# The second half's attention of a two-layer decoder: a stream of two-key-block tiles in a fixed TensorE order

## The chip, the cores and the metric

The kernel runs on one core of a Trainium2 chip. Its engines are TensorE (PE in the profile; PEld is its weight loading), VectorE (DVE), ScalarE (ACT), GpSimd (POOL) and SyncE (SP), whose queue issues nearly all DMAs of this kernel. The metric is the device time of one execution in microseconds (us), the median of several runs.

## What is computed

A decoder trunk of two layers for 1024 tokens of width 1024, all in float32: an mLSTM layer with its MLP, then a multi-head latent attention (8 heads) with its MLP. The attention shares its keys and values, and each head has a part without rotation (128) and a rotary part (64) that all heads' keys share:

```python
def block(args):
    qn_b, qr_b, start = args
    s = (jnp.einsum('bqhd,bkhd->bhqk', qn_b, k_nope)
         + jnp.einsum('bqhd,bkd->bhqk', qr_b, k_rope)).astype(jnp.float32) * scale
    qpos = start + jnp.arange(B_QBLOCK, dtype=jnp.int32)
    s = jnp.where(kpos[None, :] <= qpos[:, None], s, -jnp.inf)
    p = jax.nn.softmax(s, axis=-1)
    return jnp.einsum('bhqk,bkhd->bqhd', p.astype(v.dtype), v)
...
def sqrelu_mlp(h, w1, w2):
    return jnp.square(jax.nn.relu(h @ w1)) @ w2
```

## The kernel before

Matrix products are made of three matmuls on parts: each float32 operand is split into a rounded high part (ACT's cast) and a low part (DVE's subtraction), and `mm3` (L279 to L282) multiplies high by high, high by low and low by high. `wsplit` (L235) does this for weights that arrive by DMA in a `raw` tile, `split_mod` (L498) for results in PSUM.

The tokens are worked in two halves of 512. While one half goes through the latent attention, the MLP of the other half runs beside it. `two_streams` (L2779) weaves the two generators: it takes a step of the attention side, which says by the number it yields how many MLP steps are due, and then takes that many from the MLP side. 0 means none, 0.5 half a step. `go` (L2762) runs each step under `issue_after` the last TensorE instruction before it, so that TensorE's instructions of one step come after those of the steps before. Within a step the planner of the framework chooses the order on each engine, by priority and by its own estimate of times; `prompt` (L244) raises the priority.

An MLP step of layer 1's first half (`mlp`, L1297) is 24 matmuls of 512 columns: a hidden block of 128 (`hidden`, into a `ps` tile of PSUM) or a share of the output (`up_rows`, into `pm` tiles). Each step can stop in its middle, at `yield "within"`, and each has one 512 KB weight transfer, asked for two steps ahead (`AHEAD`).

The change is in the attention of the second half, whose queries see up to 1024 keys. Its unit is a pair of query tiles of one head (`j` = 2 or 3): the query tiles 2j and 2j+1 of 128 queries each, with `nk` = 6 or 8 key blocks of 128. For each head `loaded_head` (L1877) fetches keys, query, rotary query and values from DRAM into `k4` tiles (512 KB each). `attend_beside` (L1981) then does, in turn:

- `scores` (L1803) for both query tiles of a pair, each into a `pm` tile (two PSUM banks; there are two such tiles): `score_mm` makes five matmuls for each 512 keys and adds the causal mask; `softmax` takes the row maximum on DVE, the exponential with its row sum on ACT, the reciprocal and the scaling on DVE. Probabilities go to `raw` tiles, of which there are four, shared with the weights of the MLP.
- `turned` (L1984): TensorE transposes the probabilities of four key blocks into two `pc` tiles of PSUM, and `split_mod` splits them into two `hd` tiles (there are eight).
- `products` (L2000): these tiles times the values, summed over the key blocks in a `ps` tile, one round behind `turned`.

A pair has two rounds of up to four key blocks. In each round, products of the round before, transposes, and in the last round also the scores of the next pair form one step. The MLP steps due after the rounds are 1, 0.5 and 0.5 in rotation (L2171).

The rotary keys are the tiles `hf.kk`: high and low part, two `hd` tiles of 1024 columns for the second half, whose first halves are fetched from DRAM (L1650 to L1653) and whose second halves `latent` computes (L1688, L1689). Once the last pair's scores are done, `load_o` (L2188) fetches the outputs of heads 0 to 5 for the output projection; from head 6 on they stay in SBUF (`last_o`, L2182).

Of the kernel before, what the change touches and what calls it, by code (L numbers as in the profile page):

```python
# [9 lines left out]
F32 = mybir.dt.float32  # L10
F32R = mybir.dt.float32r
# [71 lines left out]
def kernel(  # L83
# [1528 lines left out]
    def latent(hf, behind):  # L1612
# [35 lines left out]
        for i in range(2):  # L1648
            nc.sync.dma_start(hf.cs[:, i], rope_d[i][:, ts(hf.i, H)])
        if hf.i:  # L1650
            hf.kk = [hd(F32R), hd(F32R)]
            for i in range(2):
                nc.sync.dma_start(hf.kk[i][:, 0:H].bitcast(F32), kkd[i])  # L1653
        else:
            t = hdv(F32R)
            hf.kk = [t[:, 0], t[:, 1]]
# [29 lines left out]
        kr = last_of(rp)  # L1686
        rstd_k = last_of(rs)
        nc.scalar.copy(hf.kk[0][:, s], kr)  # L1688
        nc.vector.tensor_sub(hf.kk[1][:, s], kr, hf.kk[0][:, s].bitcast(F32))  # L1689
        if not hf.i:  # L1690
            for i in range(2):
                nc.sync.dma_start(kkd[i], hf.kk[i].bitcast(F32))
# [84 lines left out]
    def score_mm(o2, kk, q, kn, i):  # L1777
# [5 lines left out]
        for g in range((n + 511) // 512):  # L1783
            w = min(512, n - g * 512)
            o = o2(g)
            ks = slice(g * 512, g * 512 + w)
            kh, kl = kn[0][:, ks], kn[1][:, ks]
            nc.tensor.matmul(o[:, :w], ql, kh, start=True, stop=False)  # L1788
            nc.tensor.matmul(o[:, :w], qh, kl, start=False, stop=False)
            nc.tensor.matmul(o[:, :w], qT, kk[1][:, ks], start=False, stop=False)  # L1790
            nc.tensor.matmul(o[:, :w], qT, kk[0][:, ks], start=False, stop=False)
            if g == i // 4:
                nc.tensor.matmul(o[:, ts(i % 4, P)], identb, maskA, start=False, stop=False)
            nc.tensor.matmul(o[:, :w], qh, kh, start=False, stop=True)  # L1794

    def softmax(f, pr, n):
        m, l = small(1), small(1)
# [180 lines left out]
                finish()  # L1978
        late()

    def attend_beside(hf, groups, dense, behind=lambda: None):  # L1981


        def turned(work):  # L1984
            PTh, PTl = hdv(F32R, 256), hdv(F32R, 256)
            n = 0
            for u, b0, nb in work:
                for b in range(b0, b0 + nb, 2):
                    pt = pc()
                    turns = [(0, b), (1, b), (0, b + 1), (1, b + 1)]  # L1990
                    if b + 2 == u.nk:
                        turns.pop(2)
                    for m, (i, kb) in enumerate(turns):
                        nc.tensor.transpose(pt[:, ts(m, P)], u.prs[i][:, ts(kb, P)], ident)  # L1994
                    s = slice(n * 256, n * 256 + len(turns) * P)
                    split_mod(flat_of(PTh)[:, s], flat_of(PTl)[:, s], pt[:, : len(turns) * P], None)
                    n += 2
            return PTh, PTl

        def products(work, PT):  # L2000
            n = 0
            for u, b0, nb in work:
                if b0 == 0:
                    u.po = ps()[:, :256]
                for kb in range(b0, b0 + nb):
                    o, at = u.po, slice(0, 256)
                    if kb == u.nk - 1:
                        o, at = u.po[:, P:], slice(0, P)
                    mm3(o, *u.v[kb], PT[0][:, n, at], PT[1][:, n, at], kb == 0, kb == u.nk - 1)
                    n += 1  # L2010
                if b0 + nb == u.nk:
                    s = ts(u.j % 2, 256)
                    if u.hh < 6:
                        o = tmp()[:, :256]
                        nc.scalar.copy(o, u.po)
                        nc.sync.dma_start(oT[ts(u.hh, P), ts(u.j, 256)], o)
                    else:
                        split_mod(hf.o.hi[u.hh][:, s], hf.o.lo[u.hh][:, s], u.po, None)

        def begin():  # L2020
            us = []
            for head, j in next(groups, []):
                u = Half()
                (u.hh, _, _, u.v), u.j, u.nk = head, j, 2 * j + 2
                u.prs = scores(hf.kk, (head, j))
                us.append(u)
            return us

        late = None
        yield "align"  # L2030
        us = begin()
        yield 1
        while us:
            if sum(u.nk for u in us) <= 4:
                rounds = [[(u, 0, u.nk) for u in us]]
            else:
                rounds = [[(u, b, min(4, u.nk - b))] for u in us for b in range(0, u.nk, 4)]
            for n, work in enumerate(rounds):
                if late:
                    late()  # L2040
                PT = turned(work)
                late = lambda a=(work, PT): products(*a)
                if len(rounds) == 1:
                    yield 1
                if n == len(rounds) - 1:
                    us = begin()
                    if not us:
                        behind()
                yield next(dense)
        late()  # L2050

    def attention_first(hf):

# [96 lines left out]
    def attention_second(hf):  # L2150
# [12 lines left out]
        def units():  # L2163
            for hh in range(NH):
# [1 line left out]
                if hh == 6:  # L2166
                    last_o(hf)
                for j in range(2, 4):
                    yield [(h_, j)]

        yield from attend_beside(hf, units(), cycle((1, 0.5, 0.5)), lambda: load_o(hf))  # L2171

    def primed(g, then):

# [771 lines left out]
```

## Time and profile before

| | |
|---|---|
| Median of 3 runs | 2295.67 us |
| Lowest, highest | 2294.85, 2296.79 us |
| Span of the profiled execution | 2291.6 us |
| VectorE busy over the span | 1691.5 us (74%) |
| ScalarE busy over the span | 1126.3 us (49%) |
| HBM read, written | 343.65 MB, 98.57 MB |

The span runs from the first to the last instruction of one profiled execution. A row of the timeline has start, duration, engine, line, operation, output tile and inputs, and, in brackets, how long the engine had been idle before it and what released it. TensorE's matmuls overlap, and the ends shown are modelled, so the distance from one start to the next is read, not the duration. In a group of the rows by form, the numbers behind the bar are busy time and the mean of one instruction in ns, then the idle time ahead of the group and its releaser.

### The profile page before, as it was taken

Reading aid. Unit: us, or ns where it says so; the run is one execution under the profiler, and the core shown is the slowest. Engines: PE = TensorE matmul, PEld = TensorE weight load, DVE = VectorE, ACT = ScalarE, POOL = GpSimd, SP = SyncE. Lnnn points to the kernel's source line nnn. Section 1 sums busy time; section 2 is a strip of 40 time slices with the busy share of each in tenths; the row PEclk is TensorE's granted clock in tenths of the full one; section 3 lists DMA queues with packets and bytes.
Section 4 is the critical chain, followed back from the end, with each engine's and each line's share of the span. In section 5 each row is a group of like instructions: output and inputs, shape, how many; then the busy total and the mean of one; then the engine's idle time right before and its main releaser. Section 6 shows DMA issues by size and latency. Waiting matters only on the chain.

```text
span 2291.6 us, 32039 instructions
## 1 busy us (share of the span) xinstructions
PE 2265.0 (99%) x11818; PEld 1904.4 (83%) x11818; DVE 1691.5 (74%) x2715; ACT 1126.3 (49%) x1915; POOL 84.3 (4%) x164
## 2 busy tenths in 40 slices
PE   8999999999999999999999999999999999999998
PEld 6888888888888878878888888888888888989997
DVE  6677767889887877687765777656666398698776
ACT  4355425865334445545444654444444354655453
POOL 1000000001122210000000000000000000000000
PEclk9999999999999999999999999999999999999999
DMA  9544454668999887666776755764434352546332
GB/s 318 184 128 131 149 166 146 204 218 267 327 280 308 280 297 267 194 221 198 246 235 202 248 189 160 245 233 149 143 102 148 106 157 83 161 142 183 117 111 111
DMA packets 399597, 444.33 MB, mean 194 GB/s; under 512 B 27123, under 2 KB 285232, under 8 KB 399440
## 3 DMA queue, kind: packets, MB, share of 16 engines
q1 hardware_dynamic: 386496, 397.09, 54.7%
q0 software_dynamic: 12944, 45.20, 5.3%
q8 instruction: 93, 1.52, 0.3%
q14 instruction: 64, 0.52, 0.1%
HBM read 343.65 MB, written 98.57 MB: 193 GB/s over the span
## 4 chain that ended last, share of the span: by engine, by line
PE 85%; DVE 5%; DMA 5%; issue 3%; ACT 2%; POOL 0%; SPq 0%; DVEq 0%; ACTq 0%; POOLq 0%
PE ps L280 14%; PE ps L281 13%; PE ps L282 13%; PE pm L281 10%; PE pm L280 10%; PE pm L282 9%; DMA raw<-in_mlp_w_dram 3%; PE pc L281 2%; PE pc L280 2%; PE pc L282 2%; PE pc L1994 1%; DVE k L247 1%; PE pm L1794 1%; DVE wl L239 1%; PE pm L1788 1%
## 5 line engine op out<-in xcount | busy, mean ns | idle before, releaser
L238 ACT CAST wh<-raw 128x1024 fp32r<-128x1024 f32 (+2 forms) x317 | 321.4, 1016 | 417.0 <-PE ps L281 187.5
L239 DVE TENSOR_TENSOR wl<-raw,wh 128x1024 fp32r<-128x1024 f32 (+2 forms) x317 | 375.3, 1186 | 196.2 <-ACT wh L238 175.8
L280 PE MATMUL ps<-k,wh 128*128 128x512 f32 (+1 forms) x1237 | 468.3, 379 | 0.3 <-ACT tmp L533 0.2
L282 PE MATMUL ps<-k,wl 128*128 128x512 f32 (+1 forms) x1237 | 462.1, 374 | 0.0
L281 PE MATMUL ps<-k,wh 128*128 128x512 f32 (+1 forms) x1237 | 461.7, 373 | 0.0
L280 PEld LDWEIGHTS ps<-k,wh 128*128 128x128 f32 x1237 | 233.1, 188 | 44.3 <-issue 3.0
L282 PEld LDWEIGHTS ps<-k,wl 128*128 128x128 f32 x1237 | 233.0, 188 | 41.5
L281 PEld LDWEIGHTS ps<-k,wh 128*128 128x128 f32 x1237 | 233.2, 188 | 40.6 <-issue 1.2
L247 DVE TENSOR_TENSOR k<-k,pm 128x512 f32<-128x512 f32 (+1 forms) x250 | 192.2, 800 | 60.2 <-PE pm L282 59.5
L280 PE MATMUL pm<-wh,hd 128*128 128x512 f32 x488 | 193.0, 395 | 1.7 <-ACT raw L1799 1.5
L282 PE MATMUL pm<-wh,hd 128*128 128x512 f32 x488 | 190.4, 390 | 0.0
L281 PE MATMUL pm<-wl,hd 128*128 128x512 f32 x488 | 190.4, 390 | 0.0
L280 PEld LDWEIGHTS pm<-wh,hd 128*128 128x128 f32 x488 | 91.7, 188 | 22.0 <-ACT raw L1799 2.5
L282 PEld LDWEIGHTS pm<-wh,hd 128*128 128x128 f32 x488 | 91.6, 188 | 19.8 <-DVE hd L502 0.5
L281 PEld LDWEIGHTS pm<-wl,hd 128*128 128x128 f32 x488 | 91.8, 188 | 18.4 <-issue 0.5
L280 PE MATMUL pm<-hd,wk 128*128 128x512 f32 x256 | 101.3, 396 | 1.4 <-ACT hd L501 1.4
L281 PE MATMUL pm<-hd,wk 128*128 128x512 f32 x256 | 100.0, 391 | 0.4 <-DVE hd L502 0.4
L280 PE MATMUL pm<-hd,wh 128*128 128x512 f32 x256 | 99.2, 389 | 0.6 <-ACT hd L501 0.6
L281 PE MATMUL pm<-hd,wh 128*128 128x512 f32 x256 | 99.6, 390 | 0.2 <-DVE hd L502 0.2
L282 PE MATMUL pc<-k,wl 128*128 128x256 f32 (+1 forms) x307 | 99.3, 323 | 0.5 <-DVE wl L239 0.5
L282 PE MATMUL pm<-hd,wk 128*128 128x512 f32 x256 | 99.7, 390 | 0.0
L282 PE MATMUL pm<-hd,wl 128*128 128x512 f32 x256 | 99.7, 390 | 0.0
(502 smaller groups left out, 4701.8 us busy)
## 6 DMA issues: line engine op xcount, KB each, us to landing
raw<-in_mlp_w_dram SPq DMA_DIRECT2D x176, 512.0 KB, 4.7
raw<-in_mlp_w_dram SPq DMA_DIRECT2D x128, 256.0 KB, 4.8
raw<-in_ada_w_dram SPq DMA_DIRECT2D x54, 512.0 KB, 4.7
raw<-in_a_w_in_dram SPq DMA_DIRECT2D x44, 512.0 KB, 4.0
lo<-wl POOLq DMA_DIRECT2D x32, 512.0 KB, 6.2
wk<-lo SPq DMA_DIRECT2D x64, 256.0 KB, 4.2
xs<-k SPq DMA_DIRECT2D x40, 256.0 KB, 4.0
hd<-in_ada_w_dram SPq DMA_DIRECT2D x18, 512.0 KB, 7.9
```

The source lines that it names most:

```text
L238: nc.scalar.copy(hi[:, :n], r[:, :n])
L239: i = nc.vector.tensor_sub(lo[:, :n], r[:, :n], hi[:, :n].bitcast(F32))
L247: return f(*a, **k)
L280: nc.tensor.matmul(o, lh, rh, start=start, stop=False)
L281: nc.tensor.matmul(o, lh, rl, start=False, stop=False)
L282: pe_last[0] = nc.tensor.matmul(o, ll, rh, start=False, stop=stop)
L1788: nc.tensor.matmul(o[:, :w], ql, kh, start=True, stop=False)
L1794: nc.tensor.matmul(o[:, :w], qh, kh, start=False, stop=True)
L1994: nc.tensor.transpose(pt[:, ts(m, P)], u.prs[i][:, ts(kb, P)], ident)
```

## The change

Five things change, all in the second half's attention:

1. The unit of transposing, splitting and multiplying is a tile of two key blocks: one `pc` tile, one `hd` tile that holds high and low part.
2. Each piece (transposes of a tile, products of a tile, scores of one query tile) is a step of its own, separated by `yield 0`, so that TensorE's order among them is the one written: transposes of a tile, products of the tile two before it, and behind the first two tiles of a pair the scores of one query tile of the next pair.
3. After each pair, instead of after each round, MLP work is due, and it is half a step.
4. The softmax takes the exponential and the scaling in two pieces, of the first 512 keys and of the rest, with a row sum each. The first query tile's probabilities lie in a `raw` tile, the second's in two `tmc` tiles.
5. The low part of the rotary keys moves from an `hd` tile to the tiles `tma` and `v7`.

```diff
         if hf.i:
-            hf.kk = [hd(F32R), hd(F32R)]
-            for i in range(2):
-                nc.sync.dma_start(hf.kk[i][:, 0:H].bitcast(F32), kkd[i])
+            low = [
+                sb.tile([P, n], F32R, tag=t, bufs=1, name=f"kk_{t}")[:, :H]
+                for t, n in (("tma", 512), ("v7", 4 * VE))
+            ]
+            hf.kk = [hd(F32R), low]
+            nc.sync.dma_start(hf.kk[0][:, 0:H].bitcast(F32), kkd[0])
+            nc.sync.dma_start(low[0].bitcast(F32), kkd[1])
...
-        nc.vector.tensor_sub(hf.kk[1][:, s], kr, hf.kk[0][:, s].bitcast(F32))
+        low = hf.kk[1][1] if hf.i else hf.kk[1][:, s]
+        nc.vector.tensor_sub(low, kr, hf.kk[0][:, s].bitcast(F32))
...
+    def score_two(st, kk, q, kn, i):
+        qn, T = q
+        qs = ts(i % 4, P)
+        qh, ql, qT = qn[:, 0, qs], qn[:, 1, qs], T[:, qs]
+        n = (i + 1) * P
+        for g, ks in enumerate((slice(0, 512), slice(512, n))):
+            w = ks.stop - ks.start
+            o, kh, kl = st[:, g, :w], kn[0][:, ks], kn[1][:, ks]
+            nc.tensor.matmul(o, ql, kh, start=True, stop=False)
+            nc.tensor.matmul(o, qh, kl, start=False, stop=False)
+            nc.tensor.matmul(o, qT, kk[1][g][:, :w], start=False, stop=False)
+            nc.tensor.matmul(o, qT, kk[0][:, ks], start=False, stop=False)
+            if g:
+                nc.tensor.matmul(o[:, w - P :], identb, maskA, start=False, stop=False)
+            nc.tensor.matmul(o, qh, kh, start=False, stop=True)
+
+    def softmax_two(f, pr, n):
+        m, l, a = small(1), small(1), small(2)
+        nc.vector.reduce_max(m, f[:, :n], axis=AX.X, negate=True)
+        for g, w in ((0, 512), (1, n - 512)):
+            nc.scalar.activation(
+                pr[g][:, :w], f[:, g * 512 : g * 512 + w], AF.Exp, bias=m, accum_out=a[:, g : g + 1]
+            )
+        nc.vector.tensor_add(l, a[:, 0:1], a[:, 1:2])
+        nc.vector.reciprocal(l, l)
+        for g, w in ((0, 512), (1, n - 512)):
+            nc.vector.tensor_scalar(pr[g][:, :w], pr[g][:, :w], l, None, ALU.mult)
...
-    def attend_beside(hf, groups, dense, behind=lambda: None):
+    def attend_beside(hf, units, dense, behind):
+        def turned(u, b):
+            t = hdv(F32R)
+            pt = pc()
+            turns = [(0, b), (1, b), (0, b + 1), (1, b + 1)]
+            if b + 2 == u.nk:
+                turns.pop(2)
+            for m, (i, kb) in enumerate(turns):
+                nc.tensor.transpose(
+                    pt[:, ts(m, P)], u.prs[i][kb // 4][:, ts(kb % 4, P)], ident
+                )
+            w = len(turns) * P
+            split_mod(t[:, 0, :w], t[:, 1, :w], pt[:, :w], None)
+            return t
+
+        def products(u, b, t):
+            if b == 0:
+                u.po = ps()[:, :256]
+            for kb in (b, b + 1):
+                last = kb == u.nk - 1
+                o = u.po[:, P:] if last else u.po
+                at = slice((kb - b) * 256, (kb - b) * 256 + (P if last else 256))
+                mm3(o, *u.v[kb], t[:, 0, at], t[:, 1, at], kb == 0, last)
...
+        def score(u, e):
+            i = 2 * u.j + e
+            st = pm()
+            score_two(st, hf.kk, u.q, u.kn, i)
+            if e:
+                pr = [tmc(), tmc()]
+            else:
+                pr = raw()
+                pr = [pr[:, 0:512], pr[:, 512:1024]]
+            prompt(softmax_two)(st.rearrange("p a b -> p (a b)"), pr, (i + 1) * P)
+            u.prs.append(pr)
+
         yield "align"
-        us = begin()
+        u = unit()
+        for e in range(2):
+            score(u, e)
         yield 1
...
+        behind_, waiting = [behind], []
+        while u:
+            then = unit()
+            for n, b in enumerate(range(0, u.nk, 2)):
+                waiting.append((u, b, turned(u, b)))
+                yield 0
+                if len(waiting) > 2:
+                    products(*waiting.pop(0))
+                    yield 0
+                if n < 2:
+                    if then:
+                        score(then, n)
+                        yield 0
+                    elif behind_:
+                        behind_.pop()()
+            yield next(dense)
+            u = then
+        for w in waiting:
+            products(*w)
...
-        yield from attend_beside(hf, units(), cycle((1, 0.5, 0.5)), lambda: load_o(hf))
+        yield from attend_beside(hf, units(), cycle((0.5,)), lambda: load_o(hf))
```

`unit()`, not shown, takes the next head and pair from `units`, with its queries, keys and values.

More of the change, by code (lines that the diff above doesn't have):

```diff
@@ L1979, in attend @@
         late()
-    def attend_beside(hf, groups, dense, behind=lambda: None):
[L1984 to L2029, printed above, removed]
@@ new lines, in attend_beside, with unit @@
+    def attend_beside(hf, units, dense, behind):
[20 more added lines that the diff above has]
+                mm3(o, *u.v[kb], t[:, 0, at], t[:, 1, at], kb == 0, last)
+            if b + 2 == u.nk:
+                s = ts(u.j % 2, 256)
+                if u.hh < 6:
+                    o = tmp()[:, :256]
+                    nc.scalar.copy(o, u.po)
+                    nc.sync.dma_start(oT[ts(u.hh, P), ts(u.j, 256)], o)
+                else:
+                    split_mod(hf.o.hi[u.hh][:, s], hf.o.lo[u.hh][:, s], u.po, None)
+        def unit():
+            g = next(units, None)
+            if g is None:
+                return None
+            u = Half()
+            (u.hh, u.q, u.kn, u.v), u.j = g
+            u.nk, u.prs = 2 * u.j + 2, []
+            return u
+        def score(u, e):
[4 more added lines that the diff above has]
+                pr = [tmc(), tmc()]
+            else:
+                pr = raw()
+                pr = [pr[:, 0:512], pr[:, 512:1024]]
+            prompt(softmax_two)(st.rearrange("p a b -> p (a b)"), pr, (i + 1) * P)
+            u.prs.append(pr)
@@ L2030, in attend_beside @@
         yield "align"
-        us = begin()
+        u = unit()
+        for e in range(2):
+            score(u, e)
         yield 1
[L2033 to L2049, printed above, removed]
@@ L2050, in attend_beside @@
-        late()
+        behind_, waiting = [behind], []
[15 more added lines that the diff above has]
+            u = then
@@ L2168, in units @@
                 for j in range(2, 4):
-                    yield [(h_, j)]
-        yield from attend_beside(hf, units(), cycle((1, 0.5, 0.5)), lambda: load_o(hf))
+                    yield h_, j
+        yield from attend_beside(hf, units(), cycle((0.5,)), lambda: load_o(hf))
     def primed(g, then):
```

## The prediction

> **What bounds the kernel now.** I read the page first, then the windows, the waits and the timeline of the stage in which the second half's attention runs. From the page:
>
> ```profile
> span 2291.6 us, 32039 instructions
> PE 2265.0 (99%) x11818; PEld 1904.4 (83%) x11818; DVE 1691.5 (74%) x2715; ACT 1126.3 (49%) x1915; POOL 84.3 (4%) x164
> ```
>
> TensorE works 99% of the span. A new order can only win what TensorE loses now. The transposes of this attention (L1994) run from 1518 to 1761 us. The windows of that stretch, of the 160 us behind it, and of its first 40 us:
>
> ```profile
> core 0: us, PE busy (x) PEld busy (x) DVE busy (x) ACT busy (x) POOL busy (x), PEclk, DMA share, GB/s
> 1518.00:1761.00 243.00, 241.51 (x1373) 207.48 (x1372) 149.22 (x226) 107.63 (x188) 0.20 (x2) 1.00 0.39 128
> 1761.00:1921.00 160.00, 160.00 (x708) 131.76 (x708) 108.90 (x146) 76.52 (x108) 0.20 (x2) 1.00 0.46 140
> 1520.00:1560.00 40.00, 38.51 (x211) 32.55 (x210) 24.93 (x37) 17.56 (x30) 0.00 (x0) 1.00 0.36 116
> ```
>
> The granted clock (PEclk) is 1.00 throughout, and all of TensorE's idle time, 1.5 us, lies in the first 40 us. Who made it wait, from the waits of the surrounding stretch (total, times, longest):
>
> ```profile
> PE pm L280 <- ACT raw L1799: 1.5, 2, 0.8
> PEld pc L1994 <- DVE raw L1801: 0.8, 4, 0.2
> ```
>
> The first row is an MLP step that wants the PSUM pair `pm` while the exponential still reads it; the second is a transpose that comes before its probabilities are normalised. The timeline shows the cause of the first:
>
> ```profile
> 1540.28 0.30 PE L1794 MATMUL pm<-k,k 128*128 128x128 f32 x1
> 1541.36 1.05 ACT L238 CAST wh<-raw 128x1024 fp32r<-128x1024 f32 x1 [4.58 <-DMA raw<-in_mlp_w_dram]
> 1542.44 1.23 DVE L239 TENSOR_TENSOR wl<-raw,wh 128x1024 fp32r<-128x1024 f32 x1 [4.83 <-ACT wh L238]
> 1543.58 0.81 DVE L1798 TENSOR_REDUCE sm<-pm 128x1 f32<-128x640 f32 x1
> 1544.23 0.37 PE L1794 MATMUL pm<-k,k 128*128 128x256 f32 x1
> 1545.37 0.50 PE L280 MATMUL pm<-wh,hd 128*128 128x512 f32 x1 [0.77 <-ACT raw L1799]
> 1547.99 0.39 PE L282 MATMUL pm<-wh,hd 128*128 128x512 f32 x1
> 1549.10 0.50 PE L280 MATMUL pm<-wh,hd 128*128 128x512 f32 x1 [0.72 <-ACT raw L1799]
> ```
>
> A weight transfer landed late, ACT's cast and DVE's subtraction waited for it in their queues, and the row maximum of scores finished at 1540.6 started only at 1543.58. Both waits follow. Start to start they cost 1.14 − 0.12 and 1.11 − 0.23, together **1.9 us**: that, the 0.8 us of the transposes and some reshuffling (below) are all there is to win here.
>
> **The change part by part.** The times that TensorE takes per instruction, as start-to-start steps, and the chain of one softmax:
>
> ```profile
> 1563.33 0.40 PE L280 MATMUL ps<-k,wh 128*128 128x512 f32 x1
> 1563.53 1.22 DVE L1798 TENSOR_REDUCE sm<-pm 128x1 f32<-128x1024 f32 x1 [0.41 <-PE pm L1794]
> 1564.02 0.39 PE L280 MATMUL ps<-k,wh 128*128 128x512 f32 x1
> 1564.25 0.39 PE L281 MATMUL ps<-k,wh 128*128 128x512 f32 x1
> 1564.85 1.12 ACT L1799 ACTIVATE raw<-pm,sm 128x1024 f32<-128x1024 f32 x1 [2.58 <-DVE sm L1798]
> 1566.09 0.16 DVE L1800 RECIPROCAL sm<-sm 128x1 f32<-128x1 f32 x1 [1.33 <-ACT raw L1799]
> 1566.18 0.27 PE L1994 MATMUL pc<-ident,raw 128*128 128x128 f32 x1
> 1566.21 0.36 PE L281 MATMUL ps<-hd,k 128*128 128x256 f32 x1
> 1566.29 0.75 DVE L1801 TENSOR_SCALAR raw<-raw,sm 128x1024 f32<-128x1024 f32 x1
> 1566.41 0.28 PE L282 MATMUL ps<-hd,k 128*128 128x256 f32 x1
> 1566.53 0.22 PE L280 MATMUL ps<-hd,k 128*128 128x128 f32 x1
> 1599.47 1.06 PE L1994 MATMUL pc<-ident,raw 128*128 128x128 f32 x8
> 1600.29 0.48 PE L280 MATMUL ps<-k,wh 128*128 128x512 f32 x1
> 1600.61 0.39 PE L281 MATMUL ps<-k,wh 128*128 128x512 f32 x1
> ```
>
> A 512-wide matmul takes 0.23 us, a 256-wide product 0.12, and eight transposes with the switch back to matmuls 0.82 + 0.32 − 0.23 = 0.91, some 0.11 each.
>
> *TensorE's work.* The score, transpose and product matmuls keep their number and widths: 0. An MLP step is 24 matmuls of 512, so 5.4 us. Before, 32 rounds take two thirds of a step each, 21.3 steps; after, 16 pairs of query tiles take half a step each, 8. So 13.3 steps, 72 us, move behind the attention, where the second window shows TensorE full. The stage should shrink from 243 to about 171 us and the rest grow by as much: 0 in sum.
>
> *The two `pm` waits.* The MLP half step no longer stands right behind both score tiles: at least one tile of transposes and products lies between, and weights are wanted every 21 us instead of every 11. I take **−1.9**; at worst a late weight does it again: 0.
>
> *Order.* Now transposes and products are shuffled into scores one by one; the product at 1566.21 behind a lone transpose took 0.20 instead of 0.12. A dozen such places, and none with the fixed order: **−1.0** (0 to −1.5).
>
> *Tiles of two key blocks.* 56 groups of transposes instead of 32. A switch costs about 0.91 − 8 × 0.11 = 0.03 us: 24 × 0.03 = **+0.7**.
>
> *Softmax.* This is the critical term. Rows by form, 1520 to 1760:
>
> ```profile
> L1799 ACT ACTIVATE raw<-pm,sm 128x1024 f32<-128x1024 f32 x8 | 8.9, 1118 | 16.2 <-DVE sm L1798 16.2
> L1799 ACT ACTIVATE raw<-pm,sm 128x640 f32<-128x640 f32 x7 | 5.6, 795 | 13.4 <-DVE sm L1798 13.4
> L1799 ACT ACTIVATION_READ_ACCUMULATOR raw<-pm,sm 128x1 f32 x30 | 5.7, 191 | 0.0
> L1801 DVE TENSOR_SCALAR raw<-raw,sm 128x1024 f32<-128x1024 f32 x8 | 6.0, 752 | 0.2
> L1801 DVE TENSOR_SCALAR raw<-raw,sm 128x640 f32<-128x640 f32 x7 | 3.8, 548 | 0.1
> L239 DVE TENSOR_TENSOR wl<-raw,wh 128x1024 fp32r<-128x1024 f32 x22 | 26.9, 1222 | 16.3 <-ACT wh L238 16.0
> L247 DVE TENSOR_TENSOR k<-k,pm 128x512 f32<-128x512 f32 x44 | 28.2, 681 | 5.0 <-PE pm L282 4.7
> ```
>
> By the lines through the two widths, a 512-wide exponential takes 0.69 us and its fixed part is 0.26; a 512-wide scaling takes 0.48, fixed part 0.21. Splitting adds 32 × (0.26 + 0.19) = 14 us to ACT and 32 × (0.16 + 0.21) = 12 us to DVE. On neither is that the bound: DVE's weight splits and accumulations for 21 MLP steps are 26.9 + 28.2 = 55 us, 2.6 a step, so the new stage holds about 149 − 55 + 12 + 8 × 2.6 = 127 us of DVE in 171 (74%, from 61%).
>
> The path counts. From the reduction's start to normalised probabilities the chain took 1563.53 to 1567.04, 3.5 us. After, the maximum 1.22, two exponentials with their sums read out 2 × 0.69 + 0.1, addition and reciprocal 0.4, the first scaling 0.48 and the hand-overs (0.1 as between DVE and ACT here) make 3.7 to the first half, which is all that the next transposes want. TensorE reaches the next instruction 0.2 ahead of the reduction, so 3.9 must be covered. Behind the last score tile (1024 keys) of a pair stand three transposes, 0.33, a tile's six products, 0.71, and 12 MLP matmuls, 2.72: **3.8 us**. For 768 keys the maximum takes about 0.95 (between the rows of 640 and 1024) and the second exponential 0.47, so the chain is 0.5 shorter and the cover a tile longer: hidden. In the fixed order nothing overtakes a waiting transpose: the older tiles' products and the next scores stand behind it. Before, the cover was as thin (12 MLP matmuls and a few products) and cost 0.8 us in all; DVE served the chain almost at once. For the eight thin places I take 0.3 each, nearest to those 0.2 waits plus the longer chain: 2.4 − 0.8 = **+1.6**. Bounds: 0 each gives −0.8; one weight split of 1.22 ahead of the chain each time gives 8 × (0.1 + 1.22) − 0.8 = +9.8.
>
> The Trainium skill, "Trace Analysis", section "Optimizing Scalar/DVE Operations", puts the fixed part of an operation at about 51 ns (ScalarE on PSUM) and 60 ns (VectorE on SBUF). By that figure, as an estimate, the split would lengthen the chain by 0.1 us instead of 0.2, and the sum would be some 0.8 us lower; the rows here show more, 0.26 and 0.21, and the sum goes by them.
>
> *Buffers.* Keys' low part moves to two tiles idle in this stage: 0. An `hd` slot comes free; three transposed tiles, four MLP tiles and the keys fill eight, so each tile waits for products that TensorE has already passed: 0.
>
> *The end.* The other heads' outputs are fetched (L2193) at the first tile of the last pair, with the pair's other tiles, its products and one and a half MLP steps (8 us) of TensorE work before the output projection wants them: 0.
>
> *Heads' loads.* A head now lasts about 21 us instead of 31. The loads go through SP's queue once their `k4` slots are free; from its rows and the DMA view of 1490 to 1770:
>
> ```profile
> 1562.71 0.80 SPq L1882 DMA_DIRECT2D k<-kd  x2
> 1713.41 1.12 SPq L1882 DMA_DIRECT2D k<-kd  x2
> k<-kd SPq DMA_DIRECT2D x14, 512.0 KB, 4.5
> ```
>
> The 1562.71 loads are head 3's, two heads on, sent when head 1's scores release their slots: still more than 20 us ahead after the change. Head 7's (1713.41) came late, as head 6 takes two slots for its output: they go with head 5's last products. In the new order 7.2 us lie between those and head 7's scores, against 1.1 of issuing and 4.5 to landing: 0 to +2 with other transfers in between, taken as **0**.
>
> **Sum:** −1.9 − 1.0 + 0.7 + 1.6 = −0.6 on a span of 2291.6. The median of the runs is 2295.67, 4.1 above the span; I carry that over: **2295.1**.
>
> **The rivals.**
> - *Slower: DVE's queue takes the place of the `pm` wait.* With half a step as cover, any weight split or accumulation in front of the maximum or the scaling stops TensorE. Against: the high priority and the 0.8 us so far. For: the 1542.44 row, and DVE's share rising to 74%. At its full price the sum is −1.9 − 1.0 + 0.7 + 9.8 = +7.6, 2303. It passes +0.2% (4.6 us) when the eight places wait 1.0 us each. Chance 0.18.
> - *Slower: heads' loads late.* If SP's queue holds keys behind another wait so that each lands 2 us late, 7 × 2 − 0.6 = +13: 2309. Chance 0.06.
> - *Faster by more than 0.2%.* All named losses of the stage are 1.9 + 0.8 + 1.5 = 4.2 us, under the 4.6 needed, so gains elsewhere would be required, while the following window is full. 2290. Chance 0.07.
> - *Headroom in TensorE itself.* Weight loads are busy 207.48 of 243 us; if the rest were free, 36 us could go: 2260. But in the window behind, TensorE is busy for 160.00 of 160 us and its loads for 131.76 (82%), so about that share is what a full TensorE looks like here. Chance 0.01. The Trainium skill, "Trace Analysis", section "Identifying the Most-Contended Engine", would have headroom read from that share rather than from matmul busy time; here the second window decides.
> - *The order was already what TensorE did.* Then nothing but position changes: 2295.7, inside the forecast.
>
> **How the numbers follow.** Within 0.2% (about what a measurement of this kernel can tell from no change) 0.68, faster 0.08, slower 0.24. The low end takes all gains and no waits, −1.9 − 1.5 − 0.8 + 0.7 = −3.5: 2292, widened to 2291 for later stages. The high end takes the first rival: 2303.
>
> **What would show it.** The last transposes near 1690 us; no wait of `pm` L280 on the exponential in the stage; TensorE's waits on the scaling about 2.4 us in some eight places; DVE busy about 74% there; keys landing before their scores. I am wrong if the waits at the eight places approach 1 us, if TensorE waits for `k` loads, or if other stages move by microseconds because the planner orders them differently.

## The result

The changed kernel takes **2325.05 us** (median of 4 runs, 2323.28 to 2326.53) against 2295.26 us (4 runs, 2294.71 to 2296.79) of the kernel before: ratio 1.0133, 95% interval 1.0119 to 1.0147. It is slower by 30 us, where 2295.1 us (2291 to 2303) had been forecast.

From the page of the changed kernel, the lines that answer to those shown of the kernel before:

```profile
span 2324.8 us, 32223 instructions
PE 2273.8 (98%) x11818; PEld 1909.8 (82%) x11818; DVE 1702.7 (73%) x2779; ACT 1134.8 (49%) x1979; POOL 85.3 (4%) x164
```

The instructions of TensorE are the same 11818, so the 30 us are waiting or slower work, not more work. The windows of the stage of the second half's attention and of the 160 us behind it (the transposes, now L2030, run from 1522.84 to 1719.26):

```profile
core 0: us, PE busy (x) PEld busy (x) DVE busy (x) ACT busy (x) POOL busy (x), PEclk, DMA share, GB/s
1523.00:1720.00 197.00, 172.55 (x1042) 149.42 (x1041) 124.25 (x241) 90.71 (x215) 0.33 (x2) 0.97 0.36 127
1720.00:1880.00 160.00, 160.00 (x710) 131.81 (x709) 103.05 (x141) 72.79 (x105) 0.20 (x2) 1.00 0.43 130
```

TensorE is idle for 197.00 − 172.55 = 24.5 us in the stage, where it was idle for 1.5, and its granted clock is 0.97 there instead of 1.00, which is another 197 × 0.03, some 6 us. Behind the stage it is full again. From the first transposes to the last matmul the kernel before took 765.0 us and this one takes 793.9: the stage holds the loss. What lies ahead of it, 4.2 us in these two executions, I take as scatter: the first transposes came between 1518.3 and 1526.6 us in the fourteen kernels that were profiled, at 1520.9 in a variant of the kernel before. So the 765.0 and its like are what I compare below, beside the measured ratios.

Who made TensorE wait, from the waits around the stage (total, times, longest):

```profile
PE pc L2030 <- DVE tmc L1831: 22.1, 8, 4.3
PE ps L280 <- DVE k L502: 1.4, 1, 1.4
PE pc L2030 <- DVE hd L502: 0.9, 1, 0.9
```

The first row is the wait that the prediction had called critical: the transposes that want the scaled probabilities of the second query tile. There are eight, one a head, as it said; but start to start they lose 23.3 us, 2.9 each and not 0.3. The timeline around one of them, that of the third head, shows how it comes about:

```profile
1549.89 0.38 SPq L260 DMA_DIRECT2D raw<-in_mlp_w_dram  x1
...
1553.36 0.55 SPq L1927 DMA_DIRECT2D k<-vd  x1
...
1556.51 1.23 DVE L239 TENSOR_TENSOR wl<-raw,wh 128x1024 fp32r<-128x1024 f32 x1 [2.47 <-ACT wh L238]
...
1565.82 0.32 SPq L2050 DMA_DIRECT2D oT<-tmp  x1
1575.63 0.32 SPq L1927 DMA_DIRECT2D k<-vd  x1
1576.05 0.39 SPq L260 DMA_DIRECT2D raw<-in_mlp_w_dram  x1
...
1578.53 1.22 DVE L1823 TENSOR_REDUCE sm<-pm 128x1 f32<-128x1024 f32 x1
...
1580.95 1.05 ACT L238 CAST wh<-raw 128x1024 fp32r<-128x1024 f32 x1 [1.89 <-DMA raw<-in_mlp_w_dram]
...
1581.85 0.27 PE L2030 MATMUL pc<-ident,raw 128*128 128x128 f32 x1
1581.90 0.68 ACT L1825 ACTIVATE tmc<-pm,sm 128x512 f32<-128x512 f32 x1
1582.03 1.23 DVE L239 TENSOR_TENSOR wl<-raw,wh 128x1024 fp32r<-128x1024 f32 x1 [1.82 <-ACT wh L238]
...
1583.17 1.28 DVE L247 TENSOR_TENSOR k<-k,pm 128x512 f32<-128x512 f32 x2
1584.37 0.15 DVE L1828 TENSOR_TENSOR sm<-sm 128x1 f32<-128x1 f32 x1
1584.55 0.16 DVE L1829 RECIPROCAL sm<-sm 128x1 f32<-128x1 f32 x1
1584.75 0.88 DVE L1831 TENSOR_SCALAR tmc<-tmc,sm 128x512 f32<-128x512 f32 x2
1585.29 0.33 PE L2030 MATMUL pc<-ident,tmc 128*128 128x128 f32 x1 [3.17 <-DVE tmc L1831]
```

Read it from below. The transposes stop at 1581.85 and go on at 1585.29. The row maximum was done at 1578.53 + 1.22 = 1579.75, but the exponential starts at 1581.90, 2.15 us later: ScalarE works in order, and ahead of the exponential stands the cast of a weight (L238) that waits for its transfer. Then VectorE does the split of that weight and two accumulations of the MLP (L247, 1.28) ahead of the sum of the row sums (L1828): the second half of the exponential and its sum were done at 1583.34 by ScalarE's rows, so about 1.0 us goes here. And why does the weight land so late? It is issued at 1576.05, right behind a transfer of values (L1927) that SyncE's queue could only issue at 1575.63, when the last products of the head before, at 1575.44, had released the values' slot. Ahead of the values the queue had already stood from 1553.91 to 1565.82 for the transfer of an output (oT, L2050), whose data ScalarE finished only then. SyncE's queue is in order too, so the weight stood behind two transfers that wait, the second of them for a buffer. The waits rows of SyncE give the sizes:

```profile
SPq L2050 <- ACT tmp L2049: 69.0, 6, 12.1
SPq L1927 <- PE ps L282: 57.1, 6, 9.5
```

For the six heads from the second to the seventh, the exponential starts 2.81, 2.16, 2.61, 1.99, 4.18 and 3.06 us behind the maximum, 16.8 together; in three of them two accumulations add 1.0 each, 2.9; the waits of TensorE are 2.99, 3.32, 2.86, 3.16, 4.42 and 4.22, 21.0. The 1.3 left, 0.2 a head, is what the prediction had priced at 0.3. In all six the same row, the cast L238, stands between maximum and exponential.

The two other heads are of another kind. In the first, 2.0 us, the weight is there, and the wait is VectorE's work: between the row sums and the scaling stand the split of a weight (L239 at 1530.87, 1.22) and two accumulations (L247 at 1532.25, 1.29). The last costs 0.35.

Theory A is that the late landing of the weights makes the loss: a cast that waits for its weight, ahead of the exponential. Theory B, the rival, is that the cover was mis-sized: the chain of the softmax is longer than 3.9 us, or VectorE's queue is too full for it with half an MLP step as cover, whatever the transfers do.

### The profile page after: what moved, and what is told of

Its sections match the earlier page's. It is cut to its first block, busy times and chain, and to the rows that moved or that the text cites. A ratio compares the mean times of both kernels' runs of the same rounds, so it can differ in the third digit from the quotient of the medians.

```text
span 2324.8 us, 32223 instructions
## 1 busy us (share of the span) xinstructions
PE 2273.8 (98%) x11818; PEld 1909.8 (82%) x11818; DVE 1702.7 (73%) x2779; ACT 1134.8 (49%) x1979; POOL 85.3 (4%) x164
## 4 chain that ended last, share of the span: by engine, by line
PE 80%; DMA 8%; DVE 7%; ACT 3%; issue 2%; POOL 0%; DVEq 0%; SPq 0%; ACTq 0%; POOLq 0%
PE ps L280 13%; PE ps L282 13%; PE ps L281 13%; PE pm L281 9%; PE pm L280 8%; PE pm L282 8%; DMA raw<-in_mlp_w_dram 4%; PE pc L282 2%; PE pc L281 2%; PE pc L280 2%; DMA raw<-s 1%; DVE k L247 1%; DVE wl L239 1%; PE pc L2030 1%; ACT wh L238 1%
## 5 line engine op out<-in xcount | busy, mean ns | idle before, releaser
L238 ACT CAST wh<-raw 128x1024 fp32r<-128x1024 f32 (+2 forms) x317 | 321.6, 1016 | 467.5 <-PE ps L281 219.7
L239 DVE TENSOR_TENSOR wl<-raw,wh 128x1024 fp32r<-128x1024 f32 (+2 forms) x317 | 374.6, 1184 | 222.9 <-ACT wh L238 205.4
L247 DVE TENSOR_TENSOR k<-k,pm 128x512 f32<-128x512 f32 (+1 forms) x250 | 192.4, 802 | 70.6 <-PE pm L282 70.1
L502 DVE TENSOR_TENSOR hd<-tmp,hd 128x512 fp32r<-128x512 f32 x112 | 78.8, 706 | 30.0 <-ACT hd L501 29.6
```

The source lines that it names most:

```text
L238: nc.scalar.copy(hi[:, :n], r[:, :n])
L239: i = nc.vector.tensor_sub(lo[:, :n], r[:, :n], hi[:, :n].bitcast(F32))
L247: return f(*a, **k)
L502: nc.vector.tensor_sub(lo, u, hi.bitcast(F32))
```

## The experiments

Twelve kernels, each timed beside the kernel before on the same chip, and each ratio is against those runs. "Wait" is the start-to-start loss at the transposes that want the scaling, "length" the time from the first transposes of the stage to the last matmul, in one profiled execution. The kernel before has a length of 765.0, the changed one 793.9.

| run | built on | ratio to before (95%) | wait, us | length, us |
|---|---|---|---|---|
| changed kernel | | 1.0133 (1.0119 to 1.0147) | 23.3 | 793.9 |
| e2_values_pool | after | 1.0031 (1.0020 to 1.0043) | 5.7 | 771.4 |
| e6_weights_pool | after | 1.0007 (0.9999 to 1.0016) | 2.0 | 769.0 |
| e5_no_mlp | after | 1.0157 (1.0137 to 1.0177) | 32.8 | 804.6 |
| e1_cover | after | 1.0015 (1.0005 to 1.0024) | 0 | 769.3 |
| e4_before_half | before | 1.0032 (1.0020 to 1.0045) | 0 | 770.8 |
| e8_end | e2 | 1.0031 (1.0020 to 1.0042) | 5.4 | 772.7 |
| e7_all | e1, e8 | 0.9997 (0.9988 to 1.0007) | 0 | 766.9 |
| e9_before_pool | before | 1.0000 (0.9991 to 1.0009) | 0 | 764.7 |
| e10_end_steps | e6 | 0.9992 (0.9983 to 1.0000) | 2.0 | 763.8 |
| e11_best | e10, e1 | 0.9981 (0.9973 to 0.9990) | 0 | 762.1 |
| e12_before_weights | before | 0.9988 (0.9979 to 0.9996) | 0.3 | 764.9 |
| e13_cover_end | e1, with the end of e10 | 0.9999 (0.9989 to 1.0008) | 0 | 765.1 |

### The values in another queue

```diff
-                nc.sync.dma_start(flat(vt[i]), vd[hh, i])
+                nc.gpsimd.dma_start(flat(vt[i]), vd[hh, i])
```

> The changed kernel with the values' loads (k<-vd) moved from SP's queue to POOL's. In the profile of the changed kernel the weight transfer stands behind such a load in SP's queue, lands while ACT's cast of it stands ahead of the exponential, and TensorE waits some 23 us in all for the scaling (8 times), after which the granted clock is about half for a few us. Theory A (late weight transfer): without the wait of the values in SP's queue the waits for the scaling fall from about 23 to under 6 us and the clock stays at 1.00, so about 2300 us. Theory B (half a step is too little cover by itself): the waits stay above 18 us and the time within 4 us of 2325.

Ratio 1.0031: 23 us of the 30 are gone, with the cover, the tiles and the chain of the softmax as they were; at 2306.08 us it is 6 us slower than theory A had expected. The waits on the scaling fall from 22.1 to 4.2 us, and six of the eight are now 0.28 to 0.42 us. The other two, 2.3 in the first head and 1.2 in the seventh, are VectorE's work again: a weight's split and two accumulations in the first, an accumulation ahead of the scaling in the seventh. The planner also ordered some casts differently here, so by itself this could be the order and not the queue. But in six heads the cast stands ahead of the exponential as before. The timeline of one:

```profile
1553.56 1.22 DVE L1823 TENSOR_REDUCE sm<-pm 128x1 f32<-128x1024 f32 x1
...
1554.01 1.05 ACT L238 CAST wh<-raw 128x1024 fp32r<-128x1024 f32 x1
1554.95 0.69 ACT L1825 ACTIVATE tmc<-pm,sm 128x512 f32<-128x512 f32 x1
...
1557.38 0.33 PE L2030 MATMUL pc<-ident,tmc 128*128 128x128 f32 x1 [0.27 <-DVE tmc L1831]
```

The weight is there, the cast waits for nothing and runs while VectorE takes the maximum, and the exponential follows 0.17 us after the maximum's end (1554.78) instead of 2 to 4; in the other five it is 0.04 to 0.17. So a cast ahead of the exponential costs next to nothing when its weight has landed. In the two heads left, the third and the fifth, the weight is still late: it lands 2.7 and 2.6 us behind the end of the maximum, as keys (L1919) now wait ahead of it in SyncE's queue, 19.0 us in these two places. But there the planner has put the cast behind the exponentials, and TensorE waits 0.28 us. The loss needs both, a late weight and its cast ahead of the exponential.

### The weights in another queue

```diff
+    wq = [nc.sync]
...
-            nc.sync.dma_start(
+            wq[0].dma_start(
                 r.rearrange("p (a b) -> p a b", b=b)[:, a0 : a0 + na, c0 : c0 + nb]
...
+        wq[0] = nc.gpsimd
         yield from attend_beside(hf, units(), cycle((0.5,)), lambda: load_o(hf))
+        wq[0] = nc.sync
```

> The changed kernel, but the weights asked for while the second half's attention runs are issued by GpSimd's queue, and the heads' values stay in SyncE's. Theory A (a weight transfer that stands behind the values in SyncE's in-order queue lands late, and ScalarE's cast, which waits for it, stands ahead of the exponential): which of the two goes to the other queue does not matter, so the transposes' waits on the scaling fall from 22.1 us to 4-6 and the time to that of the run with the values on GpSimd's queue, ratio to the kernel before 1.003 (1.001 to 1.006). Theory B (what that run won came from the planner's other order of casts and accumulations, not from the queue): waits above 12 us, ratio 1.008 or more.

Ratio 1.0007: 29 of the 30 us are gone, better than the 1.001 to 1.006 expected, and theory B as stated above falls: half a step is cover enough. (The expectation gives the letter B to another rival, that the planner's other order won and not the queue. This run can't settle that one, since in none of its heads does a weight's cast stand between maximum and exponential. In the run before, the landing alone did it in the heads with the cast ahead, and the order alone in the third and fifth.) The values stay where they were, behind their buffers in SyncE's queue; only the weights no longer stand behind them. They go out at once when the split of the weight before has released its tile; two such issues in the timeline of this run:

```profile
1533.30 0.90 POOL L261 DMA_DIRECT2D raw<-in_mlp_w_dram  x1 [29.25 <-DVE wl L240]
1553.93 0.71 POOL L261 DMA_DIRECT2D raw<-in_mlp_w_dram  x1 [19.73 <-DVE wl L240]
```

In the changed kernel the weight of 1576.05 could have gone the same way behind the split of 1556.51, 18 us earlier. All waits of TensorE around the stage in this run:

```profile
PE ps L281 <- DVE k L503: 1.4, 1, 1.4
PE pc L2031 <- DVE hd L503: 0.9, 1, 0.9
PE pc L2031 <- DVE tmc L1832: 0.2, 1, 0.2
```

The wait on the scaling has shrunk to 0.28 us start to start at six heads and 0.37 at the last, none at the first: 2.0 in all. This is the forecast's 0.3 a place: with weights in time, half a step covers the chain just as the prediction worked it out. The stage takes 169.3 us (1521.01 to 1690.31; forecast "about 171"). What is left are the two other rows, at the end of the stage.

### No cover at all

```diff
-        yield from attend_beside(hf, units(), cycle((0.5,)), lambda: load_o(hf))
+        yield from attend_beside(hf, units(), cycle((0,)), lambda: load_o(hf))
```

> The changed kernel with no MLP step between the pairs; all remaining steps come behind the attention. No weight transfer and no cast can delay the chain, so this measures the bare chain against the bare cover. Estimated 3.9 us of chain against 1.1 us of cover for 1024 keys and 3.4 against 2.1 for 768: waits of 2.8 and 1.3 us, 8 times each, 33 us, and half the clock behind many of them, so 2325 to 2345 us. If theory B holds (chain far longer than 3.9 us, about 7): waits of 5.9 and 4.4, over 80 us, 2375 us or more.

Without MLP work in the stage there are also no weights, casts and accumulations in it, so this shows the bare chain. From the waits:

```profile
PE pc L2030 <- DVE tmc L1831: 29.0, 15, 3.0
```

TensorE loses 2.97 us at six of the eight tiles of 1024 keys (2.71 and 3.16 at the first and last) and 1.20 at six of those of 768, where 2.8 and 1.3 were expected. With the three transposes and six products that still stand between (1.04), the chain is 4.0 us; the prediction had 3.9. The changed kernel, with half a step as cover, was hardly faster than this one, 1.0133 against 1.0157: of the 0.0150 that the cover gives with weights in time (e6_weights_pool), late weights had eaten 0.0126.

### More cover, and the old order with less

More MLP work behind each pair in the new order, and as little in the old one:

```diff
-        yield from attend_beside(hf, units(), cycle((0.5,)), lambda: load_o(hf))
+        yield from attend_beside(hf, units(), cycle((1.5, 1, 1.5)), lambda: load_o(hf))
```

> The changed kernel with 1.5, 1 and 1.5 MLP steps behind a pair in rotation instead of half a step, so about as much MLP work in the attention as before the change (21 steps); stream of two-key-block tiles and fixed order kept. If the stream itself costs (tiles, order, split softmax): still over 2310 us. If only thin cover behind the last scores costs (A or B): the waits for the scaling nearly vanish, 2293 to 2299 us. Theory A leaves up to 0.5 us a pair, as the cover of 6.5 us is near the 7 us of chain and late weight together.

Ratio 1.0015, 2300.12 us, 1 us above the range expected. No wait on the scaling is left, with every transfer still in SyncE's queue and six exponentials still 2.0 to 2.6 us behind their maximum. So theory A needs a second half: a late weight costs where the cover is thinner than the chain with its lateness. From its waits, two rows remain:

```profile
PE pc L2030 <- DVE hd L502: 2.6, 1, 2.6
PE pm L280 <- ACT tmc L1825: 2.5, 2, 1.3
```

The second is the wait for `pm` that the kernel before had, still alive (a late cast holds up an exponential, and the MLP wants its tile); the first is the end of the stage again.

```diff
-        yield from attend_beside(hf, units(), cycle((1, 0.5, 0.5)), lambda: load_o(hf))
+        yield from attend_beside(hf, units(), cycle((0, 0.5)), lambda: load_o(hf))
```

> The kernel before with half an MLP step per pair (0 behind the first round, 0.5 behind the second) and all else as it was: only the amount of MLP work in the attention changes. If thin cover is the cause, with late weights or without: waits for the scaling of the same kind as in the changed kernel, 2310 to 2325 us. If the fixed order of the stream is the cause: within 5 us of 2295, as the planner can still move products in front of waiting transposes.

Ratio 1.0032: the old order with half an MLP step a pair loses some 7 us, not 30, and none at the scaling. That lies between the two forecasts. Its longest wait, 3.5 us at 1683.94, is at the end of the stage. Weights are late here too: the casts sit idle for 22.9 us in ten places until one lands. But no such cast stands ahead of an exponential of 1024 keys, which follow their maximum within 0.04 us; in three heads one stands ahead of an exponential of 640 keys and delays it by 0.9 to 1.5 us, and there no transpose waits for the scaling. So thin cover and late weights alone don't make the loss; a late cast ahead of the exponential at the thin place does.

### The end of the stage

In the last pair no scores of a next pair stand between the tiles, and there `load_o` works on the other heads' outputs. From the timeline of the changed kernel:

```profile
1713.17 2.35 DVE L2245 TENSOR_TENSOR k<-raw,k 128x1024 fp32r<-128x1024 f32 x2
...
1715.44 1.28 DVE L502 TENSOR_TENSOR hd<-pc,hd 128x512 fp32r<-128x512 f32 x2
...
1716.18 0.33 PE L2030 MATMUL pc<-ident,raw 128*128 128x128 f32 x1 [0.92 <-DVE hd L502]
...
1716.64 1.22 DVE L2245 TENSOR_TENSOR k<-raw,k 128x1024 fp32r<-128x1024 f32 x1
1717.77 0.42 DVE L502 TENSOR_TENSOR k<-ps,k 128x256 fp32r<-128x256 f32 x1
...
1718.24 0.39 PE L280 MATMUL ps<-hd,k 128*128 128x256 f32 x1 [1.41 <-DVE k L502]
```

VectorE subtracts these outputs (L2245, 1.22 each) ahead of the splits of the tiles (L502), and the next transposes and products wait: 1.11 and 1.56 us start to start, 2.7 together. First I moved the call of `load_o` from the first tile of the pair to the last (on the kernel with the values in GpSimd's queue):

```diff
...
-                    elif behind_:
-                        behind_.pop()()
...
+            if not then:
+                behind_.pop()()
             yield next(dense)
```

> The kernel with the values on GpSimd's queue, and in addition the other heads' outputs are asked for at the last tile of the last pair instead of the first. Theory A (the casts and subtractions of these outputs, 1.05 and 1.22 us each, stand ahead of the splits of the last pair's tiles on ScalarE and VectorE, and cost TensorE 1.1 + 1.6 us there): these two waits go, 2.7 us less, ratio to the kernel before about 1.002 instead of 1.003. Rival: the outputs are then late for the output projection, which waits 2 us or more for them: no gain, ratio 1.003 or above.

No gain, 1.0031, and the same two waits: 1.16 and 1.56. Neither side had it: the outputs aren't late, but the subtractions still run at the same place, ahead of the splits. Where the call stands in the program doesn't set where the planner puts its work. All three edits together:

> The changed kernel with three things at once: MLP steps of 1.5, 1 and 1.5 in rotation behind the pairs instead of half a step, the values on GpSimd's queue, and the other heads' outputs asked for at the last tile of the last pair. If the losses named so far (waits on the scaling behind a thin cover, late weights, the outputs' work at the end) are all there is, what is left is the sum forecast for the fixed order, -1.9 - 1.0 + 0.7, about 2 us under the kernel before: ratio 0.999 (0.998 to 1.000). If small tiles and the fixed order cost something of their own, ratio 1.001 or more, with no wait over 1 us left in the stage.

Ratio 0.9997, a little short of the 0.999 expected, and its trace has one wait over 1 us left in the stage, at its end: 2.75 us for the splits, this time behind a weight's split and those of a hidden block. So I gave the end cover instead of moving its work, on the kernel with the weights in GpSimd's queue:

```diff
                     elif behind_:
                         behind_.pop()()
+                if not then and n in (1, 2):
+                    yield 0.5
```

> The kernel with the MLP weights on GpSimd's queue, and in the last pair of query tiles, which has no scores of a next pair between its tiles, half an MLP step (2.7 us of TensorE work) behind the second and the third tile. Theory A (the two waits of 1.1 and 1.6 us there come from tiles that stand too close behind each other while VectorE subtracts the other heads' outputs, 1.22 us each, so cover is what lacks): both waits go, TensorE loses about 2.4 us less, ratio to the kernel before 0.9995 (0.9985 to 1.0005). Rival (the added steps bring weights' casts and splits of their own to the same place, or the outputs come late for the projection): waits of the same size remain, ratio 1.0005 or more.

Ratio 0.9992 and a length of 763.8 instead of 769.0; both waits at the end are gone. With half a step a pair, the new order is now as fast as the kernel before, or 0.1% faster: its interval reaches just to 1.0000.

### A version faster than both, and what makes it so

The same with steps of 1.5, 1 and 1.5:

> The same with MLP steps of 1.5, 1 and 1.5 in rotation behind the pairs: every loss named so far is covered, the eight waits of 0.28 us too. What is then left of the working's terms is -1.9 - 0.8 - 1.0 + 0.7, 3 us under the kernel before: ratio 0.9987 (0.998 to 0.9995). If it is 1.000, no more than about 1 us of those gains is real; if TensorE shows waits over 1 us at the end of the stage, the end still lacks cover.

**2293.73 us against 2298.24**: ratio 0.9981, interval 0.9973 to 0.9990. The window of its stage:

```profile
1521.00:1758.00 237.00, 237.00 (x1363) 204.64 (x1361) 158.58 (x287) 115.66 (x249) 17.68 (x24) 1.00 0.42 138
```

TensorE is busy for all of the 237 us at full clock, and the waits around it have no row of its matmuls. The length is 762.1, 2.9 less than the kernel before, against the 3.0 of the sum −1.9 − 0.8 − 1.0 + 0.7; single lengths are a weak test of that, as the next runs show. To see whose gain it is, the queue alone on the kernel before (values, then weights; same edits as above), and the best version without the queue:

> The kernel before with the heads' values on GpSimd's queue, all else as it was. If late weights behind the values are also what made the kernel before wait for its pm tiles (1.9 us start to start), these waits go and the ratio is about 0.999. If its weights were late for another reason, no difference: 1.000.

> The kernel before with the MLP weights of the second half's attention on GpSimd's queue, all else as it was. If the changed queue alone made the best version (ratio 0.9981) fast, the two waits for the pm tiles (1.9 us) go here as well and the ratio is 0.998 to 0.999. If its gain is that of the fixed order with enough cover, this one stays at 0.9995 to 1.0005, as with the values on that queue.

> The changed kernel with MLP steps of 1.5, 1 and 1.5 in rotation behind the pairs and half a step behind the second and third tile of the last pair, and with every transfer in SyncE's queue. Theory A (a late weight costs nothing where enough TensorE work stands in front of the waiting transposes): no wait on the scaling, 0.998 to 0.999, as the best version. Rival (the queue is needed too, since a late cast then holds up pm tiles, as the 2.5 us of two waits for pm on the exponential in the first run with more cover): 2 to 3 us more than the best version, ratio 0.999 to 1.0005.

The values' queue makes no difference to the kernel before: 1.0000. The weights' queue does, 0.9988 (0.9979 to 0.9996): both waits for `pm` are gone from its trace. The best version without the queue is at 0.9999, and has the two waits for `pm` again:

```profile
PE pm L280 <- ACT tmc L1825: 2.4, 2, 1.3
```

So the queue is worth 0.1 to 0.2% in either order, more than the new order itself: between 0.9988 and 0.9981 the intervals overlap, and so they do between 1.0000 and 0.9999. Whether the new order gains anything with enough cover stays open; the lengths (764.9 against 762.1) would say 2.8 us, but each is of one execution, and they show no gain for e12_before_weights over the kernel before, where the runs do.

## Why the prediction was wrong

**The step that failed is *Softmax*, in its price for a thin place.** Its upper bound was "one weight split of 1.22 ahead of the chain each time". In six of the eight places what stood ahead was not work but a wait: ScalarE's cast of a weight that had not landed, 2 to 4.2 us, and in three of them two accumulations as well, 1.0. In the first head it was work, the split and two accumulations, 2.0. The bound had looked at VectorE's queue alone, and there at the split alone. ScalarE's queue and, behind it, SyncE's queue were the ones that mattered. The eight places cost 23.3 us, not 2.4.

**Its root is in *The two `pm` waits*.** The row at 1541.36, a cast idle for 4.58 us until a weight landed, was quoted and read rightly as the cause of both waits. The reason given why it would get better, "weights are wanted every 21 us instead of every 11", took the lateness for a matter of rate. No row was looked up for why that weight was late. SyncE's rows of the kernel before have it:

```profile
SPq L1882 <- PE pm L1789: 14.8, 1, 14.8
1530.74 0.34 SPq L1882 DMA_DIRECT2D k<-kd  x1
1532.41 0.42 SPq L260 DMA_DIRECT2D raw<-in_mlp_w_dram  x1
```

Keys had held the queue for 14.8 us until scores released their buffer. The weight went out behind them and two further transfers, and landed 8.9 us after its issue, where the median of such transfers is 4.7. It stood behind a transfer that waits for a buffer, and asking less often does nothing against that. The runs on the kernel before agree: without the values in this queue both waits stay, without the weights both go.

**The first rival had the right place, and the right cause for a small part.** It named the eight places and VectorE's work ahead of the maximum or the scaling, which is the 2.0 us of the first head and the 2.9 of the accumulations; the 16.8 of the late casts are not in it. It said that the sum would pass +0.2% when the eight places wait 1.0 us each; they waited 2.9. **The second** named SyncE's queue and a transfer held behind another's wait, but for the keys, which came in time: no wait of TensorE for `k` loads shows. The transfer that suffered was the weight, and through it the softmax.

**Point by point, the other terms.**
- *TensorE's work, 0*: right. The same instructions; 169.3 us of stage with weights in time against 171 forecast, and a full TensorE behind it (160.00 of 160).
- *The two `pm` waits, −1.9*: right in that no such row shows in the changed kernel.
- *The chain and its cover*: right. 4.0 us bare (forecast 3.9), 0.28 us a place with weights in time (forecast 0.3).
- *Order, −1.0, and small tiles, +0.7*: not separable, and not shown. The best version's length agrees with their sum, but it is one execution, and by its runs the new order gains nothing clear of noise (above).
- *The end, 0*: wrong, +2.7. It counted TensorE's work until the outputs are wanted, but not the 1.22 us subtractions among the splits of the last tiles.
- *The sum without late weights* is then −0.6 + 2.7 = +2.1, 1.0009; e6_weights_pool measured 1.0007 (0.9999 to 1.0016). That it agrees so closely is in part luck: its one length is 4.0 us over that of the kernel before.
- *VectorE at 74%*: 124.25 of 197 us, 63%. The work was nearly as forecast (127); the stage grew by its waits.
- *Carrying over 4.1 us from span to median*: the changed kernel has 0.25 there, as its profiled execution was the slowest of its four (2326.53). The two profiled executions differ by 4.2 us ahead of the stage, so that the spans differ by 33 and the medians by 30.

What was never priced is the granted clock, some 6 us of the 30 (below). *Buffers* and *heads' loads*, both 0, were right: no wait of TensorE for either shows.

## What to carry to other kernels

When a row shows an instruction idle until a transfer landed, look up when that transfer was issued and what stood before it in its queue; a rate argument says nothing until that is known. An order fixed by hand can turn a wait in another engine's queue into the bound engine's own, so price the thin places with the longest wait seen ahead of any instruction of the chain, on every engine of it, not with the longest piece of work. And put transfers that wait for a buffer in another queue than those that something urgent waits for; or keep the work on what may land late behind the urgent chain, as in the two heads of the values' run where the cast stood behind the exponentials.

## What the hardware showed unexpectedly

**A second issuing queue was worth 29 us to the changed kernel, and about 3 to the kernel before.** The Trainium skill, "DMA: Bandwidth & Descriptors", section "Issuing engines are not separate DMA queues", says that transfers of all issuing engines run on the same 16 DMA engines and that starting them from several only saves issue time, which is usually small. By that rule the weights' run would have been near 1.013; it was 1.0007. The time saved here is not that of issuing, 0.4 us a transfer on SyncE (0.7 to 0.9 on GpSimd), but of standing in order behind transfers that wait, for a buffer up to 9.5 us at a time and for an output's data up to 12.1. (The planner's order differs between the two runs, as said, so the 29 us are those of the queue with the order that came with it.)

**TensorE's clock fell behind waits of 3 us, but not behind each.** Windows of the changed kernel around three of the waits, cut at the ends of the slow stretches:

```profile
1556.29:1559.71 3.42, 0.92 (x8) 0.92 (x9) 2.43 (x5) 1.81 (x6) 0.00 (x0) 1.00 1.02 418
1559.71:1563.12 3.41, 3.41 (x14) 2.93 (x13) 0.69 (x1) 0.31 (x1) 0.00 (x0) 0.50 0.46 183
1580.19:1583.60 3.41, 1.93 (x9) 1.29 (x8) 1.59 (x3) 2.40 (x5) 0.00 (x0) 1.00 1.03 401
1583.60:1587.01 3.41, 1.72 (x12) 1.64 (x13) 2.42 (x7) 0.59 (x1) 0.00 (x0) 1.00 0.57 229
1607.49:1610.91 3.42, 1.21 (x10) 1.21 (x11) 2.36 (x5) 1.81 (x5) 0.00 (x0) 1.00 1.03 416
1610.91:1614.32 3.41, 3.41 (x14) 2.91 (x13) 0.86 (x2) 0.02 (x1) 0.00 (x0) 0.50 0.39 156
```

Behind the waits of 2.99 and 2.86 us the granted clock is 0.50 over 3.41 us, and 512-wide matmuls start 0.43 us apart instead of 0.23; behind those of 3.32 and 3.16 it stays at 1.00. Behind 4.42 and 4.22 it fell too. So a stall costs more than its length, and which ones do isn't set by length alone. The four slow stretches of the stage start at 1559.71, 1610.91, 1662.11 and 1689.41, which is 15, 15 and 8 times 3.413 us apart: they lie on one grid. In the 3.41 us ahead of each, TensorE is busy for 0.92, 1.21, 0.09 and 0.01 us. The waits of 3.32 and 3.16 us lie across a line of that grid, so that the stretches on both sides have 1.6 to 2.2 us of work, and the clock stays. In the other traces of this stage, too, a full-clock stretch of such a grid with at most 1.42 us of work is followed by half clock, and one with 1.62 or more by full clock; between them both occur (1.54 in e5_no_mlp, then full clock; 1.57 in e2_values_pool, then half). The Trainium skill, "TensorE: Matmul & The Clock Gate", section "What's actually happening", has the clock halve after an idle window of about 3.4 us, in windows that run freely. That the windows run freely and the phase decides agrees with these rows; that a whole window of idleness is needed does not, as windows with 0.92 and 1.21 us of work had the same effect.
